# A hybrid decoder layer on one core: w_down with more row pairs in seven products, and sums of weights made by accumulating DMAs

## The chip, the cores and the metric

The kernel runs on one core of one Trainium2 chip. The metric is the device time of one execution in microseconds; the median of three runs of the kernel before is 1053.51 us (1053.41 to 1053.66). TensorE (PE) multiplies, VectorE (DVE), ScalarE (ACT) and GpSimd (POOL) prepare its operands and take up its results, and SyncE (SP) issues nearly all DMAs. All arithmetic is in float32. A product in that precision is made of three matmuls: each operand is split into a high part (a cast to the float32r type) and a low part (the rest), and high × high, high × low and low × high are added.

## The reference

One decoder layer over x of shape (1, 256, 2048): a mixer with two attention groups, then a GeGLU block. Cut to its frame:

```python
h = rmsnorm(x, pre_mix_g)
proj = h @ w_in                               # 2048 x 4368
o_a = swa_sink_attention(q_a, k_a, v_a, sinks)        # 16 heads, window 128, ALiBi, sinks
o_b = forgetting_attention(q_b, k_b, v_b, log_f)      # 16 heads, forget gates
mix = concat(rmsnorm(o_a), rmsnorm(o_b)) @ w_out      # 2048 x 2048
x = x + rmsnorm(mix, post_mix_g)
h = rmsnorm(x, pre_ffn_g)
u = causal_dwconv(h @ w_up, conv_w, conv_b)           # 2048 x 11264, width 3
gate, val = split(u, 2)
y = (gelu(gate) * val) @ w_down                       # 5632 x 2048
x = x + rmsnorm(y, post_ffn_g)
```

The change is about the last product, y, with K = 5632 (44 row blocks of 128), 256 tokens (two blocks of 128) and 2048 columns (four blocks of 512).

## The kernel before, in words

**The stages in time.** Input projection and attention fill the first 240 us, w_out the time to about 340 us. The feed-forward block runs in two halves of 22 row blocks of w_down each: up-projections (359 to 577 us, then w_down's first half to 688 us; up-projections to 928 us, then w_down's second half to the end).

**The weights' path.** A unit of weights, 128 x 1024 float32 (512 KB), is loaded by SP into one of five `raw` buffers (`w_load`, line 69 on). ScalarE casts it to the high part, VectorE subtracts to get the low part (`split`, lines 319 to 321; `w_split`, lines 119 and 122); both parts stand in one of five `wpair` buffers until TensorE has used them. A load waits for its buffer's last reader, a split for its load and its buffer, TensorE for the split.

**w_down.** In each half, 11 pairs of row blocks meet two pairs of column blocks (n = 0 and n = 2). A plain pair (`four`, line 1132, once for each of the two column blocks) makes the eight block products of a 2 x 2 by 2 x 2 block product. A pair in seven products (`seven`, line 1084) makes seven by Winograd's form of Strassen's algorithm: it multiplies sums of blocks of the activations with sums of blocks of the weights and folds the products into y afterwards (`fold`, line 1139). Each block product is three matmuls of 512 columns (`products`, line 1070; its matmul is line 1072).

The table `SEVENS` has an entry for each half and column pair; its length is how many of the 11 pairs go in seven products, and each number says beside which plain pair that one is placed. If two stand at one place, the first half of the first one comes ahead of the plain pair, its other half behind it, and the second one follows whole.

**The sums of activations** are made by POOL when a group of the up-projection is done (lines 1030 to 1033), split, and kept in `sums` (a 4096-column tile, tag "x") with the rest in the tile `more` (tag "gb1").

**The sums of weights** of a pair come about in two ways. On the spot: `seven` loads the four blocks as `top` and `low`, and after w11, w21 and w22 have been split, VectorE makes four sums in place (line 1105), which are split in turn. Or out of DRAM: for the pairs in `STORED`, `stage` (line 909) loads the four blocks during the up-projections in two halves of 256 columns, VectorE makes the sums with four subtractions of 256 columns (line 928), and SP stores them to a DRAM tile `t_dram`. `seven` then loads three of the original blocks and all four sums, the second half of the sums into a buffer of its own, "two" (tag "gb0"), outside the last stage.

**The order of the work.** TensorE's order is written out. `tick()` counts places in TensorE's program, and `later(n, f)` has f issue its instructions n ticks on. There are 8 ticks in a projection, 2 in each unit of w_out (8 in each chunk of 512 columns), and 12 in each of the three parts of the value projection. The other engines' orders are set by a planner, except where instructions are held to the program's order (`keep_in_program_order`) and in stages where all of an engine's order is written out. Each engine runs its instructions in order, and SP's DMA instructions wait in order too.

**Where things live.** The tag "y" is a place of 4096 columns, used in turn by the scratch rows of attention (`scr`), w_out's result (`mix_sb`), four rooms for staging in the first half (`four_of`), and `y_sb`. Three buffers `u` take the up-projection's rows ahead of the convolution.

Of the kernel before, what the change touches and what calls it, by code (L numbers as in the profile page):

```python
# [27 lines left out]
SEVENS = (((0, 0, 1, 1, 2, 2), (0, 0, 1, 1, 2, 2)), ((0, 0, 1, 1, 2), (0, 1, 2)))  # L28
STORED = (((0, 0, 1), (0, 0, 3), (0, 0, 5), (0, 2, 1), (0, 2, 3), (0, 2, 5), (1, 0, 1)), ((1, 0, 3), (1, 2, 0), (1, 2, 1), (1, 2, 2)))
# [5 lines left out]
def hybrid_layer(ctx: ExitStack, tc: tile.TileContext, x, pre_mix_g, w_in, b_forget, sinks,  # L35
# [28 lines left out]
    def later(n, f):  # L64
        todo.setdefault(now[0] + n, []).append(f)
# [257 lines left out]
    with tc.tile_pool(name="mixp", bufs=1) as mp:  # L323
# [33 lines left out]
        scr = main.tile([P, 2 * D], F32, tag="y", name="scr")  # L357
        rowk, rowq, dist, u0, u1 = (scr[:, i * 256:(i + 1) * 256] for i in range(5))
        rot = [0]

        def scratch():
            rot[0] += 1
            i = 6 + rot[0] % 10
            return scr[:, i * 256:(i + 1) * 256]
# [38 lines left out]


# [262 lines left out]
        def cumsum():  # L667
# [3 lines left out]
            cT = scr[0:H, 1280:1536]  # L671
# [33 lines left out]
        mix_sb = main.tile([P, 2, D], F32, tag="y", name="mix_sb")  # L705
        mix = [[mix_sb[:, t, n * 512:(n + 1) * 512] for n in range(4)] for t in range(2)]
# [146 lines left out]
    with tc.tile_pool(name="ffn", bufs=1) as fp:  # L853
# [22 lines left out]
        NU = 3  # L876
# [3 lines left out]
        fp.tile([P, 8], F32, tag="gap", name="gap")  # L880
# [3 lines left out]
        def rows_of(b):  # L884
            u = ubuf[cnt[0] % NU]
            cnt[0] += 1
            if type(b) is list:
                for m, x in enumerate(b):
                    c = fp.tile([P, 256], F32, tag="cs", bufs=1, name="cs")
# [17 lines left out]
        in_dram = {}  # L907

        def stage(half, n, u, start, step, room):

            k = half * FHALF + u * 2
            t = in_dram[half, n, u] = tc.dram_tile([P, 4, 512], F32, name="t_dram")
            src = w_down[k * P:(k + 2) * P, n * 512:(n + 2) * 512].rearrange(
                "(a p) (b c) -> p a b c", p=P, b=2)
            for i, j in enumerate((slice(0, 256), slice(256, 512))):
# [8 lines left out]
                def add(b=b):  # L924
                    b11, b12, b21, b22 = (b[0][:, i, :] for i in range(4))
                    for y, p, q in ((b11, b12, b11), (b12, b22, b12), (b22, b22, b11),
                                    (b21, b21, b22)):
                        tc.keep_in_program_order(dve.tensor_tensor(y, p, q, op=ALU.subtract))
# [49 lines left out]
        for half in range(2):  # L978
# [5 lines left out]

            def sums_at(u):
                w, at = 384 if u < least else 512, 768 * min(u, least) + 1024 * max(u - least, 0)
                if not u:
                    sums.append(main.tile([P, 4096], F32R, tag="x", name="sums"))
# [318 lines left out]
```

## Time and profile before

| | |
|---|---|
| median of three runs | 1053.51 us (1053.41 to 1053.66) |
| the profiled execution | 1053.3 us, its span 1051.4 us |
| mean granted TensorE clock | 0.997 |
| TensorE busy | 1040.0 us, 99% |
| VectorE, ScalarE, GpSimd busy | 80%, 60%, 16% |
| read from HBM, written | 221.86 MB, 15.75 MB |
| DMA | 227 GB/s over the span, 69.5% of 16 engines on SP's queue |

The time of an execution is a little longer than the span between the first and the last instruction. A group line gives line, engine, operation, output<-inputs, shapes and count, then busy us and the mean ns of one, then the engine's idle time just before it and what ended that. "TensorE busy" counts matmuls whose ends are modelled and which overlap; how dense the work is, the distance between their starts tells. A row by stages gives the stage, its length, the busy time of PE, PEld (weight loads), DVE, ACT and POOL with their counts of instructions, the granted clock, the mean busy share of the 16 DMA engines and the GB/s that they moved.

### The profile page before, as it was taken

The numbers are of one execution on the slowest core, as the hardware profiler recorded it, in microseconds if no ns is written. First come the engines' busy times: TensorE is split into PE (matmuls) and PEld (weight loads), VectorE is DVE, ScalarE is ACT, GpSimd is POOL, SyncE is SP. The second block draws the span as 40 slices with busy tenths as digits, with TensorE's granted clock in tenths as the row PEclk, the third lists the DMA queues.
The fourth block names the chain that finished last, engine by engine and source line by source line (L and its number), as shares of the span: only waits on it lengthen the run. The fifth ranks groups of instructions, "written<-read, shape, count | busy, mean of one in ns | idle before, by whom it ended". The sixth has DMA issues, their size and how long they took to land.

```text
span 1051.4 us, 19021 instructions
## 1 busy us (share of the span) xinstructions
PE 1040.0 (99%) x7240; PEld 958.0 (91%) x7240; DVE 837.2 (80%) x1365; ACT 626.9 (60%) x1025; POOL 166.5 (16%) x210
## 2 busy tenths in 40 slices
PE   9999999999999999999999999999999999999996
PEld 7899988888888999999999888899999999988886
DVE  5999877887467888888877988967788777799783
ACT  6777757667557655555555655645565455566561
POOL 3253245441122210100000000000111000000023
PEclk9999999999999999999999999999999999999998
DMA  8645557555874878888875886777677776767783
GB/s 292 199 129 168 182 159 214 164 180 171 294 248 153 255 252 294 287 264 273 283 232 170 263 269 226 244 233 239 220 235 246 226 244 219 236 216 246 244 306 115
DMA packets 187335, 238.98 MB, mean 227 GB/s; under 512 B 8268, under 2 KB 154988, under 8 KB 186348
## 3 DMA queue, kind: packets, MB, share of 16 engines
q1 hardware_dynamic: 186924, 237.37, 69.5%
q8 instruction: 57, 0.93, 0.3%
q10 hardware_dynamic: 320, 0.40, 0.1%
q14 instruction: 34, 0.28, 0.1%
HBM read 221.86 MB, written 15.75 MB: 226 GB/s over the span
## 4 chain that ended last, share of the span: by engine, by line
PE 90%; DVE 4%; ACT 2%; DMA 1%; POOL 1%; issue 1%; SPq 0%; DVEq 0%; POOLq 0%; ACTq 0%
PE bank_att L300 23%; PE bank_acc L300 21%; PE bank_acc L1072 15%; PE bank_acc L317 12%; PE bank_acc L263 5%; PE bank_att L1072 5%; PE bank_acc L270 3%; DVE wpair L122 1%; PE bank_att L317 1%; POOL scr L450 1%; PE bank_att L518 1%; DMA raw<-in_w_in_dram 1%; PE bank_att L483 1%; PE bank_att L527 1%; DMA x_in<-in_x_dram 1%
## 5 line engine op out<-in xcount | busy, mean ns | idle before, releaser
L122 DVE TENSOR_TENSOR wpair<-raw,wpair 128x1024 fp32r<-128x1024 f32 (+3 forms) x317 | 383.6, 1225 | 116.9 <-ACT wpair L119 115.8
L119 ACT CAST wpair<-raw 128x1024 fp32r<-128x1024 f32 (+3 forms) x316 | 320.3, 1032 | 155.6 <-issue 62.6
L300 PE MATMUL bank_att<-hT,wpair 128*128 128x256 f32 x2112 | 241.2, 276 | 0.0
L300 PEld LDWEIGHTS bank_att<-hT,wpair 128*128 128x128 f32 x2112 | 240.4, 188 | 0.2
L300 PE MATMUL bank_acc<-hT,wpair 128*128 128x256 f32 x1920 | 219.2, 276 | 0.0
L300 PEld LDWEIGHTS bank_acc<-hT,wpair 128*128 128x128 f32 x1920 | 218.3, 188 | 0.0
L1072 PE MATMUL bank_acc<-wpair,G 128*128 128x512 f32 x636 | 153.5, 389 | 0.0
L1072 PEld LDWEIGHTS bank_acc<-wpair,G 128*128 128x128 f32 x636 | 119.1, 188 | 24.5
L263 PE MATMUL bank_acc<-hT,wpair 128*128 128x512 f32 x384 | 94.9, 394 | 0.0
L263 PEld LDWEIGHTS bank_acc<-hT,wpair 128*128 128x128 f32 x384 | 69.5, 188 | 13.2
L317 PE MATMUL bank_acc<-wpair,oT 128*128 128x512 f32 x336 | 78.0, 391 | 0.0
L317 PEld LDWEIGHTS bank_acc<-wpair,oT 128*128 128x128 f32 x336 | 62.6, 188 | 12.8
L1030 POOL TENSOR_TENSOR s<-yy 128x128 f32<-128x128 f32 x11 | 7.5, 681 | 408.1 <-DVE yy L1019 408.1
L320 ACT CAST wpair<-raw 128x1024 fp32r<-128x1024 f32 (+1 forms) x54 | 48.0, 892 | 36.2 <-PE bank_acc L1072 17.6
L321 DVE TENSOR_TENSOR wpair<-raw,wpair 128x1024 fp32r<-128x1024 f32 (+1 forms) x54 | 55.0, 1023 | 14.3 <-ACT wpair L320 13.4
L899 ACT ACTIVATE yy<-u,cw 128x256 f32<-128x256 f32 x88 | 48.4, 596 | 20.4 <-DVE u L894 15.3
L270 PE MATMUL bank_acc<-hT,wpair 128*128 128x256 f32 x384 | 49.4, 280 | 0.0
L270 PEld LDWEIGHTS bank_acc<-hT,wpair 128*128 128x128 f32 x384 | 47.4, 188 | 1.4
L317 PE MATMUL bank_acc<-wpair,hT 128*128 128x384 f32 (+1 forms) x288 | 47.7, 321 | 0.0
L317 PEld LDWEIGHTS bank_acc<-wpair,hT 128*128 128x128 f32 x288 | 45.4, 188 | 0.1
L320 ACT CAST G<-yy 128x256 fp32r<-128x256 f32 x44 | 16.0, 406 | 46.8 <-POOL yy L1031 23.9
L901 DVE SCALAR_TENSOR_TENSOR yy<-u,cw,yy 128x256 f32<-128x256 f32 x88 | 39.1, 482 | 2.4 <-ACT yy L899 2.2
(253 smaller groups left out, 1204.9 us busy)
## 6 DMA issues: line engine op xcount, KB each, us to landing
raw<-in_w_up_dram SPq DMA_DIRECT2D x176, 512.0 KB, 4.6
raw<-in_w_down_dram SPq DMA_DIRECT2D x68, 512.0 KB, 5.1
raw<-in_w_in_dram SPq DMA_DIRECT2D x51, 512.0 KB, 5.3
raw<-in_w_out_dram SPq DMA_DIRECT2D x32, 512.0 KB, 4.1
staged<-in_w_down_dram SPq DMA_DIRECT2D x44, 256.0 KB, 5.5
t_dram<-staged SPq DMA_DIRECT2D x22, 512.0 KB, 3.2
raw<-t_dram SPq DMA_DIRECT2D x14, 512.0 KB, 3.7
raw<-in_w_in_dram SPq DMA_DIRECT2D x16, 384.0 KB, 3.4
```

The costliest lines, as they stand in the source:

```text
L119: i1 = act.copy(hi[:, cs], raw[:, cs])
L122: i2 = dve.tensor_tensor(lo[:, cs], raw[:, cs], hi[:, cs].bitcast(F32), op=ALU.subtract)
L263: pe.matmul(b, hi[:, a, m * P:(m + 1) * P], hT[:, kt, 0:512], start=(kt == 0), stop=(last == (0, kt)))
L270: pe.matmul(b[:, 256:512], lo[:, a, m * P:(m + 1) * P], hT[:, u * 4 + a, 0:256], start=False, stop=(last == (1, u * 4 + a)))
L300: pe.matmul(b[:, m * 256:(m + 1) * 256], ws[:, a, m * P:(m + 1) * P], hT[:, kt, i * 256:(i + 1) * 256], start=not begun, stop=last == (low ...
L317: pe.matmul(b, a, r[:, cols], start=(first and i == 0), stop=(last and i == 2))
L320: act.copy(hi, src)
L321: dve.tensor_tensor(lo, src, hi.bitcast(F32), op=ALU.subtract)
L450: pool.tensor_tensor(dst, dst, row, op=ALU.mult)
L899: act.activation(y, u[:, 2:258], AF.Identity, bias=cw[:, 3, ch:ch + 1], scale=cw[:, 2, ch:ch + 1])
L901: dve.scalar_tensor_tensor(y, u[:, 1:257], cw[:, 1, ch:ch + 1], y, op0=ALU.mult, op1=ALU.add)
L1072: pe.matmul(b, x, r, start=b not in opened and not i, stop=closes and i == 2)
```

## The change

- `SEVENS`: 8, 8, 6 and 3 pairs in seven products instead of 6, 6, 5 and 3. In the first half four sevens stand at each of the first two places.
- 19 of these 25 take the weights' sums from DRAM, instead of 11 of 20. Ten (`MADE`, all of the first half) are staged as before, but 7 ticks apart instead of 10, in three rooms instead of four, and with three additions instead of four subtractions. The second half stages nothing any more.
- Nine (`ADDED`: seven of the second half, and the eighth pair of each column pair of the first) are made without an engine's arithmetic: SP copies the four blocks from w_down into the DRAM tile with two DMAs, and three DMAs issued from POOL add (`accum_op`) first the blocks' second column onto the first, then one sum onto a block, then that onto another. The steps are 8 ticks apart, the nine chains 17, from early in attention on.
- The form of the algorithm has its signs changed, so that the weights' sums are sums only; the differences go to POOL's sums of activations and to `fold`. The count of instructions there stays the same.
- The place of y is two tiles, of 3072 columns (tag "y") and of 1024 ("yb"); scratch, mix and y go through a helper, `y_place`. The first half's eighth sum of activations stands in "yb", the seventh (and the second half's sixth) in a new tile "gb2".
- Two buffers `u` instead of three; the tiles "cs" and "last" take the tag "s"; the tile "gap" is 16 columns instead of 8.

```diff
-SEVENS = (((0, 0, 1, 1, 2, 2), (0, 0, 1, 1, 2, 2)), ((0, 0, 1, 1, 2), (0, 1, 2)))
-STORED = (((0, 0, 1), (0, 0, 3), (0, 0, 5), (0, 2, 1), (0, 2, 3), (0, 2, 5), (1, 0, 1)), ((1, 0, 3), (1, 2, 0), (1, 2, 1), (1, 2, 2)))
+SEVENS = (((0, 0, 0, 0, 1, 1, 1, 1), (0, 0, 0, 0, 1, 1, 1, 1)), ((0, 0, 1, 1, 2, 2), (0, 1, 2)))
+MADE = tuple((0, n, u) for n in (0, 2) for u in (0, 1, 3, 4, 6))
+ADDED = tuple((1, 0, u) for u in (1, 3, 4, 5)) + tuple((1, 2, u) for u in range(3)) + ((0, 0, 7), (0, 2, 7))
...
+        def added(at, start):
+            t = in_dram[at] = tc.dram_tile([P, 4, 512], F32, name="t_dram")
+            src = corners(*at)
+            def copy():
+                for a in range(2):
+                    tc.keep_in_program_order(sp.dma_start(t[:, 2 * a:2 * a + 2, :], src[:, a]))
+            def add(to, what):
+                return lambda: tc.keep_in_program_order(
+                    pool.dma_start(to, what, accum_op=ALU.add))
+            for d, f in ((0, copy), (8, add(t[:, 0:2, :], src[:, :, 1, :])),
+                         (16, add(t[:, 3, :], t[:, 0, :])), (24, add(t[:, 2, :], t[:, 3, :]))):
+                later(start + d, f)
+        for i, at in enumerate(ADDED):
+            added(at, 12 + i * 17)
...
-        NU = 3
+        NU = 2
...
-                    b11, b12, b21, b22 = (b[0][:, i, :] for i in range(4))
-                    for y, p, q in ((b11, b12, b11), (b12, b22, b12), (b22, b22, b11),
-                                    (b21, b21, b22)):
-                        tc.keep_in_program_order(dve.tensor_tensor(y, p, q, op=ALU.subtract))
+                    x = b[0]
+                    for y, p, q in ((x[:, 0:2], x[:, 0:2], x[:, 1:4:2]),
+                                    (x[:, 3], x[:, 3], x[:, 0]), (x[:, 2], x[:, 2], x[:, 3])):
+                        tc.keep_in_program_order(dve.tensor_tensor(y, p, q, op=ALU.add))
...
-                    pool.tensor_tensor(s1, a21, a22, op=ALU.add)
+                    pool.tensor_tensor(s1, a21, a22, op=ALU.subtract)
                     pool.tensor_tensor(s2, s1, a11, op=ALU.subtract)
-                    pool.tensor_tensor(s4, a12, s2, op=ALU.subtract)
+                    pool.tensor_tensor(s4, a12, s2, op=ALU.add)
...
-                        start = stage(*at, start, 19 if half else 10, room)
+                        start = stage(at, start, 7, lambda: rooms.append(rooms[0]) or rooms.pop(0))
...
-                    for y, p, q in ((b11, b12, b11), (b12, b22, b12), (b22, b22, b11),
+                    for y, p, q in ((b11, b11, b12), (b12, b12, b22), (b22, b22, b11),
                                     (b21, b21, b22)):
-                        made = dve.tensor_tensor(y, p, q, op=ALU.subtract)
+                        made = dve.tensor_tensor(y, p, q, op=ALU.add)
...
-                    dve.tensor_tensor(y12, d, y22, op=ALU.add)
+                    dve.tensor_tensor(y12, d, y22, op=ALU.subtract)
                     dve.tensor_tensor(y21, f, y22, op=ALU.add)
-                    dve.tensor_tensor(y22, d, y21, op=ALU.add)
+                    dve.tensor_tensor(y22, d, y21, op=ALU.subtract)
```

More of the change, by code (lines that the diff above doesn't have):

```diff
@@ L354, in x_square, with y_place, at @@
                                    accum_out=sqx[t][:, c:c + 1]))
-        scr = main.tile([P, 2 * D], F32, tag="y", name="scr")
-        rowk, rowq, dist, u0, u1 = (scr[:, i * 256:(i + 1) * 256] for i in range(5))
+        def y_place(name):
+            parts = {}
+            def at(t, cs):
+                f, n = t * D + cs.start, cs.stop - cs.start
+                i = f >= 3 * UNIT
+                if i not in parts:
+                    parts[i] = main.tile([P, (1 if i else 3) * UNIT], F32, tag="yb" if i else "y",
+                                         name=name)
+                f -= 3 * UNIT * i
+                return parts[i][:, f:f + n]
+            return at
+        scr = y_place("scr")
+        rowk, rowq, dist, u0, u1 = (scr(0, slice(i * 256, (i + 1) * 256)) for i in range(5))
         rot = [0]
@@ L704, in hybrid_layer @@
         later(stages(5, 1)[2] + 5, lambda: group_rstd(1, rstd_b))
-        mix_sb = main.tile([P, 2, D], F32, tag="y", name="mix_sb")
-        mix = [[mix_sb[:, t, n * 512:(n + 1) * 512] for n in range(4)] for t in range(2)]
+        mix_at = y_place("mix_sb")
+        mix = [[mix_at(t, slice(n * 512, (n + 1) * 512)) for n in range(4)] for t in range(2)]
         def out_half(half, evac, chunks):
@@ L905, in conv, with stage @@
             return y
[L907 to L914, printed above, removed]
+        def stage(at, start, step, room):
+            t = in_dram[at] = tc.dram_tile([P, 4, 512], F32, name="t_dram")
+            src = corners(*at)
             for i, j in enumerate((slice(0, 256), slice(256, 512))):
@@ L1039, in hybrid_layer @@
                     split(*parts, s[:, :w])
-                if not g:
-                    if half:
-                        room = lambda: fp.tile([P, 4, 256], F32, tag="gb0", name="staged")
-                    else:
-                        four_of = main.tile([P, 4, 4, 256], F32, tag="y", name="staged")
-                        rooms = [four_of[:, i] for i in range(4)]
-                        room = lambda: rooms.append(rooms[0]) or rooms.pop(0)
+                if not half and not g:
+                    three_of = main.tile([P, 3 * UNIT], F32, tag="y", name="staged")
+                    rooms = [three_of[:, i * UNIT:(i + 1) * UNIT].rearrange(
+                        "p (a c) -> p a c", a=4) for i in range(3)]
                     start = 0
-                    for at in STORED[half]:
-                        start = stage(*at, start, 19 if half else 10, room)
+                    for at in MADE:
+                        start = stage(at, start, 7, lambda: rooms.append(rooms[0]) or rooms.pop(0))
             if half == 1:
@@ L1096, in seven @@
                 s2, s3, s4, s1 = [
-                    [x[:, i * P:i * P + P] for x in sums[1 + u]] if i < 3 or u >= least
-                    else parts_of(u * 2, 1) for i in range(4)]
+                    sums_of(u, i) if i < 3 or u >= least else parts_of(u * 2, 1)
+                    for i in range(4)]
                 (w11,) = split_into(w_parts(UNIT, held=False), top, 1)
@@ L1273, in hybrid_layer @@
                 r = rstd_y(1, 4, v)
-            gained(last if h else y_sb[:, 1, 1536:1792], b1[h], halves[h])
+            gained(last if h else y_at(1, slice(1536, 1792)), b1[h], halves[h])
         for i, n in enumerate((512, 512, 512, 256, 256)):
```

56 lines of the change are left out of this document (35 added, 21 removed).

## The prediction

> **What bounds the kernel now.** I read the page's busy shares first, then the chain of waits, then a table of busy time by stage, then the groups of single stages. The first two lines are the page's; the rest is the chain in order of time (start, length, what).
>
> ```profile
> span 1051.4 us, 19021 instructions
> ...
> PE 1040.0 (99%) x7240; PEld 958.0 (91%) x7240; DVE 837.2 (80%) x1365; ACT 626.9 (60%) x1025; POOL 166.5 (16%) x210
> ```
>
> ```profile
> 359.35 21.79 PE bank_att L300 x192
> 381.14 21.76 PE bank_acc L300 x192
> ...
> 648.40 6.80 PE bank_acc L1072 x30
> 655.20 2.04 PE bank_att L1072 x9
> ```
>
> TensorE sets the end nearly everywhere. From 359 us on, each pair of up-projections takes 21.76 us for 192 matmuls, again and again, and in the w_down stage 30 matmuls of 512 columns take 6.80 us: 0.2267 us each, with no gap between the pieces. So a matmul of w_down removed is worth 0.2267 us, and any stall that the change creates is paid in full. What counts then is how much room the engines that feed TensorE have. The table by stage shows it (columns: stage, its length, busy time of PE, PEld, DVE, ACT and POOL with instructions, clock, DMA share, GB/s):
>
> ```profile
> 128.00:240.00 112.00, 111.63 (x699) 96.39 (x698) 90.78 (x190) 75.13 (x162) 52.83 (x65) 1.00 0.58 180
> 240.00:320.00 80.00, 80.00 (x381) 66.45 (x380) 49.73 (x75) 47.09 (x80) 13.19 (x11) 1.00 0.68 230
> 320.00:359.00 39.00, 38.33 (x272) 35.15 (x271) 32.35 (x73) 29.45 (x73) 8.84 (x13) 1.00 0.67 219
> 359.00:577.00 218.00, 218.00 (x1923) 217.95 (x1922) 181.66 (x288) 121.45 (x171) 17.72 (x26) 1.00 0.79 256
> 403.00:446.00 43.00, 43.00 (x382) 43.00 (x381) 36.85 (x59) 24.33 (x34) 5.25 (x8) 1.00 0.85 276
> ...
> 490.00:533.00 43.00, 43.00 (x382) 43.00 (x381) 34.67 (x57) 23.71 (x32) 0.00 (x0) 1.00 0.88 282
> 555.00:577.00 22.00, 22.00 (x195) 22.00 (x195) 17.42 (x27) 11.45 (x16) 0.00 (x0) 1.00 0.46 153
> 577.00:688.50 111.50, 111.50 (x494) 92.32 (x494) 99.80 (x113) 68.36 (x74) 0.00 (x0) 1.00 0.77 255
> ...
> 984.00:1006.00 22.00, 22.00 (x99) 18.22 (x98) 16.61 (x18) 15.31 (x21) 0.00 (x0) 1.00 0.78 273
> ```
>
> VectorE is at 90% in w_down's first half (99.80 of 111.50 us) and at 83% in the up-projections before it (181.66 of 218). The DMA engines are at 0.85 to 0.88 while sums are staged (403 to 533 us) and at 0.58 to 0.68 in attention and w_out. Everything keeps up, and two resources have 10 to 15% left.
>
> **What it removes.** A pair in seven products does one block product less than a pair in eight, and a block product is 3 matmuls. SEVENS goes from 6+6+5+3 = 20 pairs to 8+8+6+3 = 25: 5 × 3 × 0.2267 = 3.40 us off TensorE, 2.72 of it in the first half, 0.68 in the second. The number of folds stays four, with the same number of instructions.
>
> **What it adds on VectorE and ScalarE in w_down.** The rows of that stage (line, engine, operation, shapes, count, busy us, mean ns):
>
> ```profile
> L321 DVE TENSOR_TENSOR wpair<-raw,wpair 128x1024 fp32r<-128x1024 f32 x18 | 22.0, 1222 | 7.6 <-ACT wpair L320 7.1
> ...
> L321 DVE TENSOR_TENSOR wpair<-raw,wpair 128x512 fp32r<-128x512 f32 x11 | 7.5, 685 | 0.0
> ...
> L1105 DVE TENSOR_TENSOR raw<-raw 128x512 f32<-128x512 f32 x5 | 3.5, 690 | 0.1
> ```
>
> A pair in seven with sums from DRAM splits one piece of 512 columns and three of 1024: 0.69 + 3 × 1.22 = 4.35 us of VectorE per 21 × 0.2267 = 4.76 us of TensorE. With sums made on the spot four additions of 0.69 come on top: 7.1 us. A plain pair costs 2 × 1.22 = 2.44 us per 24 × 0.2267 = 5.44 us. Per column pair of the first half the change turns two plain pairs into sevens (+2 × 1.91 us) and makes two pairs on the spot instead of three (-2.76 us): +1.06 us. Twice that gives 99.8 + 2.1 = 101.9 us of VectorE in 111.5 - 2.7 = 108.8 us of TensorE: 94%. It still fits, but the sevens now stand four to a group, with only one plain pair beside them: three from DRAM, one on the spot, one plain make 3 × 4.35 + 7.1 + 2.44 = 22.6 us of VectorE in 24.5 us. The five buffers of split weights let VectorE run about one seven ahead; a seven on the spot overdraws its own 4.76 us by 2.3, and the next seven from DRAM returns only 0.4. In the middle of a group that lead covers it: nothing. The first group also carries the tail of the last up-projection:
>
> ```profile
> 577.00:592.60 15.60, 15.60 (x70) 12.89 (x70) 15.13 (x22) 11.63 (x15) 0.00 (x0) 1.00 0.82 277
> 592.60:607.60 15.00, 15.00 (x68) 12.43 (x67) 13.24 (x15) 9.62 (x11) 0.00 (x0) 1.00 0.79 259
> ```
>
> The same mixture of pairs took 15.13 us with that tail and 13.24 without: 1.9 us. On 22.6 that makes 24.5 of 24.5 us. Its bounds are 0 and 1.9; I take 0, since the sevens that open the group now come from DRAM.
>
> **The second half of the loaded sums** goes into one buffer, "two", so its load is issued only when the one before has been split, and all later loads queue behind it on SP. Timeline, chain and DMA issues (median us to landing) of before:
>
> ```profile
> 600.84 1.06 ACT L320 CAST wpair<-two 128x1024 fp32r<-128x1024 f32 x1 [0.26 <-PE bank_att L1072]
> ...
> 601.93 1.23 DVE L321 TENSOR_TENSOR wpair<-two,wpair 128x1024 fp32r<-128x1024 f32 x1
> ...
> 603.18 0.33 SPq L74 DMA_DIRECT2D two<-t_dram  x1
> ```
>
> ```profile
> 602.84 1.36 PE bank_acc L1072 x6
> 604.20 2.04 PE bank_att L1072 x9
> ```
>
> ```profile
> raw<-t_dram SPq DMA_DIRECT2D x14, 512.0 KB, 3.7
> ...
> two<-t_dram SPq DMA_DIRECT2D x8, 512.0 KB, 6.2
> ```
>
> The issue at 603.18 follows the split's end at 603.16. TensorE reads that piece in the last 3 of the 9 matmuls, from 605.56: 2.4 us later. Before, two such sevens never stood side by side in the first half; now the seventh and the eighth pair do, in both column pairs. The next use comes 4.76 us after, so 2.4 + 4.76 less cast (1.06) and split (1.23) leaves 4.9 us for the landing. Measured are 3.7 and 6.2: late by 0 to 1.3 us, twice. The 6.2 was behind another load; here the loads ahead of it are issued earlier, so I take 0.3 twice: 0.6 us. With the first group, the bounds of the whole w_down stage are 0 and 4.5.
>
> **DMA in w_down.** A seven from DRAM loads 1.75 MiB (1.84 MB) per 4.76 us, one on the spot or a plain pair 1.05 MB. The new group moves 3 × 1.84 + 2 × 1.05 = 7.6 MB in 24.5 us: 311 GB/s. The stage's row prices the engines at 255 / 0.77 = 331 GB/s: 94%. In 984 to 1006 us 273 GB/s cost nothing. I add nothing.
>
> **Staging in the up-projections.** Ten pairs (20 half steps) instead of seven, all in the first half, a half step every 7 ticks instead of 10; a tick is 1.36 us there (16 in 21.76).
>
> ```profile
> L928 DVE TENSOR_TENSOR staged<-staged 128x256 f32<-128x256 f32 x56 | 24.1, 429 | 1.0
> ...
> L321 DVE TENSOR_TENSOR sums<-s,sums 128x384 fp32r<-128x384 f32 x5 | 2.8, 558 | 0.9 <-ACT sums L320 0.9
> ```
>
> VectorE: three additions (0.69 for the one of 512 columns, two of 0.43) 20 times are 31.0 us instead of 24.1, and two more splits of sums 1.1: 189.7 of 218 us, 87%. DMA: 1.05 MB per half step over 9.5 us instead of 13.6 is 110 GB/s instead of 77; beside the weights' 524 KB per 2.72 us, 193 GB/s, that makes 303 GB/s where 276 to 282 took 0.85 to 0.88, that is 320 to 325 GB/s at full share: 94%. Rooms come round after 21 ticks, five ticks (6.8 us) after their store, which lands in 3 us. I take nothing; if the 6% weren't there, a missing 3% of 190 us would be 5.7. The second half loses its staging, 8 × 1.72 us of VectorE, which gains nothing, since TensorE sets that stage.
>
> **The sums made by DMA.** Nine pairs: two copies of 512 KB on SP, then three accumulating DMAs on POOL's queue (512, 256, 256 KB), 8 ticks apart, each waiting for the one before; 18 and 27 issues, between 60 and 320 us. No accumulating DMA and no DMA on POOL's queue is in the trace. Nearest rows:
>
> ```profile
> t_dram<-staged SPq DMA_DIRECT2D x22, 512.0 KB, 3.2
> ```
>
> ```profile
> L450 POOL TENSOR_TENSOR scr<-scr 128x256 f32<-128x256 f32 x22 | 24.4, 1131 | 56.7 <-DVE scr L449 36.5 <-DVE rs L505 20.2
> ...
> L587 POOL TENSOR_SCALAR p<-cb,cq 128x256 f32<-128x256 f32 x16 | 12.5, 784 | 2.3 <-DMA cb<-c_dram 2.3
> ```
>
> At 230 / 0.68 = 338 GB/s the 1.05 MB copied take all engines 3.1 us. The 1.05 MB added take at least as long and, as two reads and a write, at most three times that, 9.3. A chain starts every 17 ticks: 29.8 us in attention (64 ticks in 112 us), 23.1 in w_out. So the share rises there from 0.58 to 0.79 to 1.00, in w_out from 0.68 to 0.95 to 1.22. I take the store's price (lower end), since it is the nearest row: then it fits, and costs nothing on the path. On POOL an issue costs between SP's 0.33 and a tensor operation's 1.13 us: 9 to 31 us over 260, beside 52.83 of 112 busy. Behind a POOL DMA that waits stand the multiplications of q and k (L450) and the tables (L587), which the scores need; but POOL idled 56.7 us ahead of L450 alone, and 8 ticks are 11 to 14 us where a 512 KB transfer lands in 3 to 6. Nothing again.
>
> [...]
>
> **Nothing else.** Two buffers u instead of three: a buffer is written again a whole up-projection (10.88 us) after its convolution. Scratch, mix and y in two tiles, and "cs" in "s", change names and dependencies of work long done.
>
> **Sum.** Span 1051.4 - 3.4 + 0.6 = 1048.6. The profiled run took 1053.3, 1.9 outside the span: 1050.5. The median of the runs, 1053.51, lies 0.2 above it: 1050.7 us.
>
> **Rivals.**
> 1. *w_down takes most of it back.* Groups of four sevens overrun VectorE or wait for "two". For it: 94% of VectorE, 94% of DMA, adjacency. Against: no gap at 90% before. Price 2 to 4 us: 1052 to 1054.
> 2. *The accumulating DMAs starve TensorE (slower).* In w_out the share passes 1 once the additions take more than about 4.3 us a chain (0.68 × 23.1 + 3.1 + 4.3 = 23.1). At 9.3 us the surplus is 0.22 × 80 = 18 us of DMA work; the five raw buffers of 512 KB hold 7.8 us of it at 338 GB/s, and 10 remain: 1053.5 - 3.4 + 0.6 + 10 = 1060.7. [...] A POOL that waits for late additions in attention would cost as much through the scores.
> 3. *Staging at 7 ticks saturates the DMA engines* from 360 to 550 us: up to 5.7 us, 1056.4. For and against it stands the fullest stretch of before:
>
> ```profile
> 381.00:403.00 22.00, 22.00 (x197) 22.00 (x196) 19.62 (x33) 12.05 (x18) 2.43 (x4) 1.00 0.96 306
> ```
>
> Little lies above 306 GB/s, but TensorE had no gap in it.
> 4. *Nothing comes off TensorE.* Then 1053.5; against it stands the constant 0.2267.
>
> **How the numbers follow.** A measurement tells about 0.2% from no change, 2.1 us: faster is below 1051.4, slower above 1055.6. Forecast 0.52 (1050.1 to 1051.4), rival 1 0.21, rival 2 0.16 (0.03 of it near no change), rival 3 0.10 (half slower), rival 4 0.01. Faster 0.52, same 0.21 + 0.03 + 0.05 + 0.01 = 0.30, slower 0.13 + 0.05 = 0.18. The gain can't exceed 3.4 us, so the range begins at 1049.8 with the runs' scatter; it ends at 1056.5, where rival 3 does and rival 2 mostly lies beyond. The likeliest case alone: 1049.8 to 1051.4.
>
> **What would show it.** Right: w_down's first half 2.7 us shorter, its matmuls still 0.2267 us apart; 21.76 us per pair of up-projections; DMA share below 0.95 from 240 to 320 us; accumulating DMAs that land within 8 ticks. Wrong: TensorE gaps between the last two sevens of a column pair (rival 1), ScalarE waiting for raw or POOL for t_dram before 320 us (rival 2), ScalarE waiting for raw between 360 and 550 us (rival 3).

## The result, and the profile after

The changed kernel takes 1080.43 us in the median of four runs (1077.53 to 1084.63); the kernel before, on the same chip, 1053.53 (1053.41 to 1053.66). The ratio is 1.0258, with a 95% interval of 1.0218 to 1.0299: 2.6% slower, where 0.3% faster was forecast. The profiled execution took 1078.17 us. The page of after:

```profile
span 1076.5 us, 19099 instructions
...
PE 1046.6 (97%) x7225; PEld 959.6 (89%) x7225; DVE 835.2 (78%) x1338; ACT 632.2 (59%) x1038; POOL 198.4 (18%) x248
...
q0 software_dynamic: 5040, 9.44, 5.8%
...
PE 67%; DVE 11%; DMA 10%; ACT 4%; issue 4%; POOL 3%; SPq 0%; DVEq 0%; POOLq 0%; ACTq 0%
```

The q0 line is new: the packets of POOL's DMAs. The chain that sets the end now runs for a tenth of the span through DMAs. Where the 25 us were lost, one row tells: that of the up-projection matmuls of one of its two banks, which begins with the first half's up-projections and ends with the second half's (ns min/median/max, then first and last start in us). Before, then after:

```profile
L300 PE MATMUL bank_att<-hT,wpair x2112: 276/276/282, 359.2 to 927.6; 128*128 128x256 f32 x192
```

```profile
L301 PE MATMUL bank_att<-hT,wpair x2112: 276/276/282, 376.9 to 952.9; 128*128 128x256 f32 x192
```

Three parts of the span follow, and all later runs are read in this way. The **front** (projections, attention, w_out) ends at the first start: 376.9 - 359.2 = 17.7 us later. The **middle** (both up-projections and w_down's first half) lasts from first to last start: 576.0 us, not 568.4. The **end** (w_down's second half) is the rest of the span: 123.6, not 123.8. In the chain of after the middle splits again:

```profile
377.06 21.79 PE bank_att L301 x192
398.85 21.76 PE bank_acc L301 x192
...
551.17 21.76 PE bank_att L301 x192
```

The up-projections keep their 21.76 us, so the middle's 7.6 us, and the 2.7 that should have come off there, were lost in w_down's first half. The stages by busy time (columns as before) show the same two places:

```profile
128.00:240.00 112.00, 107.79 (x658) 92.76 (x657) 84.08 (x181) 70.37 (x152) 53.80 (x68) 0.97 0.86 239
240.00:357.00 117.00, 109.21 (x555) 92.02 (x553) 70.18 (x119) 66.61 (x131) 34.73 (x37) 0.96 0.80 234
...
421.00:490.00 69.00, 69.00 (x611) 69.00 (x610) 61.85 (x94) 38.21 (x55) 8.47 (x12) 1.00 0.94 303
490.00:545.00 55.00, 55.00 (x488) 55.00 (x486) 49.44 (x79) 29.83 (x43) 7.95 (x12) 1.00 0.93 310
...
595.00:714.00 119.00, 111.97 (x483) 89.38 (x482) 99.89 (x113) 71.64 (x82) 0.00 (x0) 1.00 0.79 264
```

TensorE idles 12.0 of 229 us in the front and 7.0 of 119 in w_down, and not at all while sums are staged, although the DMA engines stand at 0.93 and 0.94 there. In the front the granted clock is 0.97 and 0.96.

### The profile page after: what moved, and what is told of

Its sections match the earlier page's. It is cut to its first block, busy times and chain, and to the rows that moved or that the text cites. A ratio compares the mean times of both kernels' runs of the same rounds, so it can differ in the third digit from the quotient of the medians.

```text
span 1076.5 us, 19099 instructions
## 1 busy us (share of the span) xinstructions
PE 1046.6 (97%) x7225; PEld 959.6 (89%) x7225; DVE 835.2 (78%) x1338; ACT 632.2 (59%) x1038; POOL 198.4 (18%) x248
## 3 DMA queue, kind: packets, MB, share of 16 engines
q0 software_dynamic: 5040, 9.44, 5.8%
## 4 chain that ended last, share of the span: by engine, by line
PE 67%; DVE 11%; DMA 10%; ACT 4%; issue 4%; POOL 3%; SPq 0%; DVEq 0%; POOLq 0%; ACTq 0%
PE bank_att L301 22%; PE bank_acc L301 20%; PE bank_acc L1119 8%; PE bank_acc L318 5%; PE bank_acc L264 3%; DVE wpair L123 3%; DMA t_dram<-in_w_down_dram 3%; DMA two<-t_dram 3%; DMA raw<-in_w_out_dram 3%; DVE wpair L322 2%; PE bank_att L1119 2%; PE bank_acc L271 2%; PE bank_att L318 1%; ACT wpair L120 1%; POOL scr L493 1%
## 5 line engine op out<-in xcount | busy, mean ns | idle before, releaser
L123 DVE TENSOR_TENSOR wpair<-raw,wpair 128x1024 fp32r<-128x1024 f32 (+3 forms) x307 | 375.0, 1239 | 116.0 <-ACT wpair L120 114.9
L120 ACT CAST wpair<-raw 128x1024 fp32r<-128x1024 f32 (+3 forms) x306 | 307.8, 1031 | 122.9 <-issue 43.2
L1119 PE MATMUL bank_acc<-wpair,G 128*128 128x512 f32 x546 | 135.5, 390 | 1.8 <-DVE wpair L322 1.0
L1119 PEld LDWEIGHTS bank_acc<-wpair,G 128*128 128x128 f32 x546 | 101.9, 188 | 24.2 <-DVE wpair L123 1.8
L321 ACT CAST wpair<-raw 128x1024 fp32r<-128x1024 f32 (+1 forms) x72 | 63.6, 900 | 44.2 <-DMA raw<-t_dram 8.6
L322 DVE TENSOR_TENSOR wpair<-raw,wpair 128x1024 fp32r<-128x1024 f32 (+1 forms) x72 | 73.2, 1035 | 17.7 <-ACT wpair L321 17.7
L1119 PE MATMUL bank_att<-wpair,G 128*128 128x512 f32 x141 | 40.6, 393 | 1.6 <-DVE wpair L322 1.4
```

The costliest lines, as they stand in the source:

```text
L120: i1 = act.copy(hi[:, cs], raw[:, cs])
L123: i2 = dve.tensor_tensor(lo[:, cs], raw[:, cs], hi[:, cs].bitcast(F32), op=ALU.subtract)
L321: act.copy(hi, src)
L322: dve.tensor_tensor(lo, src, hi.bitcast(F32), op=ALU.subtract)
L1119: pe.matmul(b, x, r, start=b not in opened and not i, stop=closes and i == 2)
```

## The experiments

What ends the waits in the front? POOL's timeline of after (start, length, idle time before and its releaser), its row among the waits, and the chain:

```profile
163.33 0.87 POOL L439 DMA_DIRECT2D t_dram<-t_dram  x1 [6.14 <-DMA t_dram<-in_w_down_dram]
...
255.09 0.86 POOL L439 DMA_DIRECT2D t_dram<-t_dram  x1 [7.70 <-DMA t_dram<-in_w_down_dram]
```

```profile
POOL t_dram L439 <- DMA t_dram<-in_w_down_dram: 24.8, 4, 9.8
...
ACT keys L321 <- POOL scr L493: 24.3, 8, 9.6
...
PE bank_att L526 <- ACT keys L321: 8.1, 2, 5.1
```

```profile
148.29 14.75 DMA t_dram<-in_w_down_dram
163.33 0.87 POOL t_dram L439
164.20 0.77 POOL scr L493
165.45 2.93 PE bank_att L526 x24
...
246.22 8.58 DMA t_dram<-in_w_down_dram
255.09 0.86 POOL t_dram L439
```

The first addition of this chain takes 14.75 us to land; POOL stands before the second one, behind it the multiplication of keys (L493), behind that ScalarE's cast of them, and then TensorE's scores. So for the front there were two theories: **POOL's waits** (a late addition holds the keys behind it: L493 follows at 164.20, after a wait of 6.14 us), and **the additions' DMA time** (weights arrive late, whoever waits). For w_down there were three: the single buffer **"two"**, VectorE's **additions on the spot** inside the groups of sevens, and the ring of five **raw** buffers.

All runs in one table: total in us, ratio to before with its 95% interval, and the three parts of the profiled execution. "No chains" means that the nine chains are left out and their pairs read other sums. The runs of one of these kernels lie 1 to 7 us apart, those of before 2.1 at most, and the profiled execution is one of them: x1 (no chains), x2 (copies only) and x13 (plain copies spread) run the same w_down code and have middles of 581.7, 579.7 and 578.6, the changed kernel 576.0. A difference in the middle of less than some 6 us is therefore read from the totals. Only after, x3, x4, x14, b1 and b2 compute the whole layer; the other kernels leave work out or put other work in its place. x15, x16, x17 and b2 ran on another chip than the other experiments; each ratio is to the kernel before on the same chip, which took 1053.45 to 1053.56 in every series.

| run | total (lowest to highest) | ratio [95%] | front | middle | end |
|---|---|---|---|---|---|
| before | 1053.53 (1053.41 to 1053.66) | | 359.2 | 568.4 | 123.8 |
| after | 1080.43 (1077.53 to 1084.63) | 1.0258 [1.0218, 1.0299] | 376.9 | 576.0 | 123.6 |
| x1_no_chains | 1066.09 (1063.45 to 1068.63) | 1.0119 [1.0100, 1.0137] | 360.5 | 581.7 | 124.7 |
| x2_copies_only | 1063.93 (1061.39 to 1064.98) | 1.0095 [1.0080, 1.0110] | 359.9 | 579.7 | 123.6 |
| x3_spread | 1071.00 (1070.37 to 1074.80) | 1.0178 [1.0159, 1.0197] | 367.5 | 577.8 | 123.4 |
| x5_plain_copies | 1073.96 (1070.58 to 1075.05) | 1.0182 [1.0157, 1.0207] | 370.7 | 578.2 | 124.4 |
| x13_spread_plain | 1063.35 (1060.97 to 1067.60) | 1.0098 [1.0064, 1.0132] | 359.6 | 578.6 | 124.2 |
| x4_two_buffers | 1073.77 (1070.98 to 1075.01) | 1.0188 [1.0173, 1.0204] | 378.2 | 571.2 | 123.4 |
| x9_no_spot_sums | 1055.08 (1053.65 to 1058.12) | 1.0017 [1.0007, 1.0026] | 359.6 | 569.7 | 123.3 |
| x8_low_elsewhere | 1067.84 (1065.65 to 1071.57) | 1.0128 [1.0109, 1.0146] | 360.0 | 582.0 | 127.9 |
| x11_two_low | 1067.84 (1065.27 to 1069.30) | 1.0132 [1.0113, 1.0151] | 359.8 | 578.9 | 128.9 |
| x12_spot_first | 1072.62 (1070.01 to 1074.64) | 1.0174 [1.0156, 1.0192] | 359.7 | 587.7 | 125.5 |
| x14_spread_first | 1078.76 (1076.94 to 1082.02) | 1.0244 [1.0219, 1.0269] | 366.8 | 584.4 | 124.0 |
| x15_first_two | 1051.88 (1050.69 to 1055.30) | 0.9987 [0.9978, 0.9996] | 359.7 | 570.8 | 123.1 |
| x16_first_raw | 1065.95 (1065.31 to 1066.67) | 1.0116 [1.0102, 1.0130] | 358.4 | 582.6 | 123.8 |
| x17_two_nosum | 1052.44 (1051.29 to 1054.04) | 0.9987 [0.9978, 0.9997] | 360.7 | 568.5 | 123.1 |
| b1_best | 1066.22 (1064.71 to 1068.52) | 1.0123 [1.0107, 1.0140] | 360.5 | 582.5 | 123.7 |
| b2_two | 1053.41 (1051.33 to 1054.84) | 0.9995 [0.9986, 1.0004] | 359.7 | 567.2 | 123.2 |

### The front: chains left out, or only their copies

```diff
# x1_no_chains
-        for i, at in enumerate(ADDED):
-            added(at, 12 + i * 17)
+                    for k, at in enumerate(ADDED):       # after the staging of MADE
+                        in_dram[at] = in_dram[MADE[k]]
# x2_copies_only: each chain is only its two copies
+            for d, f in ((0, copy),):
```

> The changed kernel without its nine chains: neither the copies on SP nor the accumulating DMAs on POOL. Those nine pairs read the sums of the first nine staged pairs instead, so their part of y is not the layer's. Everything from the up-projections on is the same work. Both theories of the first part (A: POOL waits in its order for an accumulating DMA that lands late, and q and k behind it reach the scores late; B: the chains take the DMA bandwidth that the weights need) expect the 17.7 us lost before the up-projections to vanish. If the 10.2 us lost in w_down's first half (119.1 us instead of 108.8) has causes of its own, 1060 to 1063 us, with w_down's first half still at 117 to 120 us. If the chains cause that one too, 1050 to 1051 us.

> The changed kernel with the copies on SP (9.4 MB) but without the 27 accumulating DMAs, so nine pairs use unsummed blocks of weights and y is not the layer's. A: no POOL wait, so the first part is as in the kernel before: 1060 to 1063 us. B, if the copies count: they are about a third of the chains' DMA time, so a third or more of the 17.7 us stays: 1066 us or more.

Without chains the front is back to 360.5, with SP's copies alone 359.9, both within 1.3 us of before. So the copies cost nothing there that can be told, and POOL's DMAs cost all the rest. The middle stays as slow: w_down's loss does not come from the chains. Both totals lie above the 1060 to 1063 us expected, since w_down lost more than the 10.2 us of the changed kernel's profiled execution.

### The front: later steps, or plain copies in the additions' place

```diff
# x3_spread: steps 16 ticks apart instead of 8
-            for d, f in ((0, copy), (8, add(...)), (16, add(...)), (24, add(...))):
+            for d, f in ((0, copy), (16, add(...)), (32, add(...)), (48, add(...))):
# x5_plain_copies: the same DMAs on POOL's queue, without the addition
-                    pool.dma_start(to, what, accum_op=ALU.add))
+                    pool.dma_start(to, what))
# x13_spread_plain: both
```

> The whole layer; the steps of a chain are 16 ticks apart instead of 8, the same DMAs of the same size. A: a DMA of POOL's queue then finds its forerunner landed (it takes 8.6 to 14.8 us where 16 ticks are 22 to 28), POOL does not wait, and at most 3 of the 17.7 us stay: 1061 to 1066 us. B: the bytes per time are nearly the same, so at least half of it stays: 1069 us or more.

> The changed kernel with the 27 DMAs on POOL's queue as plain copies: same places, sizes and waits, but they overwrite instead of adding, so nine pairs use blocks instead of sums and y is not the layer's. F: it is the adding (a second read of the destination) that makes them slow and costly: the software queue's share falls from 5.8% to about 3% (1.05 MB a chain at a copy's 3.1 us instead of 6.9), the 512 KB ones land in 5 to 7 us instead of 8.6 to 14.8, POOL hardly waits, and the part before the up-projections comes to within 4 us of the kernel before: 1063 to 1068 us. [...]

> Steps 16 ticks apart and plain copies instead of accumulating ones (nine pairs use blocks instead of sums). In the part before the up-projections the changed kernel loses 17.7 us, with spread steps 8.3, with plain copies 11.5, without additions 0.7. If the loss is POOL's waits plus the DMA time of the additions, this one has neither the first nor half of the second: 0 to 4 us remain, total 1060 to 1067. If SP and POOL issues or the copies' bandwidth make the rest, 7 or more remain: 1069 or more.

End of the front in us, before 359.2:

| | steps 8 ticks apart | 16 apart |
|---|---|---|
| DMAs that add | 376.9 (+17.7) | 367.5 (+8.3) |
| the same DMAs as plain copies | 370.7 (+11.5) | 359.6 (+0.4) |

Each theory had its part, and neither is the whole. With both causes away the loss is gone; each alone still costs 8.3 or 11.5 us. These are single profiled executions, but the medians of the totals say the same: after is 9.4 us above x3 and 6.5 above x5, and x13 is 7.7 below x3 and 10.6 below x5. In x5 POOL still waits, though its DMAs of 512 KB land in 7.0 us in the median, not 11.5 (waits up to the end of w_out, and the queue's row):

```profile
POOL t_dram L439 <- DMA t_dram<-in_w_down_dram: 20.7, 4, 6.5
...
ACT keys L321 <- POOL scr L493: 19.4, 8, 7.7
```

```profile
q0 software_dynamic: 2736, 9.44, 3.1%
```

The queue's rows give the price of the addition. After: 5.8% of 1076.5 us are 62.4 us of all 16 engines for nine chains, 6.9 us a chain. As plain copies the same 9.44 MB take 3.1% of 1073.3 us, 3.7 a chain. An addition costs 1.9 times a copy, 62.4 against 33.3 us for all nine chains.

In x3 POOL's additions wait 8.4 us in all, where in after it is 50.7 (10.6 of them put down to a load of w_out); what is left is late weights. Its stages, and its chain in w_out:

```profile
128.00:240.00 112.00, 109.96 (x685) 93.54 (x684) 88.83 (x186) 74.67 (x160) 58.35 (x72) 1.00 0.90 256
240.00:357.00 117.00, 112.83 (x600) 95.08 (x600) 78.09 (x136) 72.28 (x149) 30.97 (x31) 1.00 0.82 244
```

```profile
276.06 16.93 DMA raw<-in_w_out_dram
...
295.42 11.01 DMA raw<-in_w_out_dram
```

A load of w_out lands after 11 and 17 us. Its median in the whole trace, 4.1 us before, tells the same of after:

```profile
raw<-in_w_out_dram SPq DMA_DIRECT2D x32, 512.0 KB, 7.1
...
t_dram<-in_w_down_dram POOLq DMA_DIRECT2D x9, 512.0 KB, 11.5
```

The mean share in x3 is 0.90 and 0.82, not 1: TensorE starves at less than a full mean. The work comes in clusters: from 280 to 300 us the share is 1.07 and 1.02 in stretches of 10 us, for 287 and 231 GB/s, and in the next 10 us TensorE is busy for 7.33. In x13 the same bytes without the arithmetic make 0.83 and 0.78, and TensorE is as busy as before in both stages; the first one's row:

```profile
128.00:240.00 112.00, 111.58 (x701) 96.54 (x700) 91.40 (x190) 74.95 (x161) 58.19 (x76) 1.00 0.83 248
```

### w_down: one buffer "two", and what stands in a group

The chain of after goes through "two" five times within 90 us (three of them shown):

```profile
608.41 0.61 DVE raw L1152
609.05 0.70 DVE low L1152
609.77 0.70 DVE low L1152
...
615.68 1.23 DVE wpair L322
616.92 6.59 DMA two<-t_dram
...
677.31 6.93 DMA two<-t_dram
...
697.75 6.60 DMA two<-t_dram
...
704.44 1.05 ACT wpair L321
705.52 1.24 DVE wpair L322
```

One buffer is free again after load, cast (1.05) and split (1.24), so a round takes 8.9 to 9.2 us in the three shown (the other two loads took 5.81 and 5.48), where two sevens from DRAM side by side need one every 4.76 us. The first lines show how the causes meet: the third pair's additions (L1152) stand on the chain ahead of the split that frees "two" at 616.91, and only then is the fifth pair's load issued.

```diff
# x4_two_buffers (the whole layer): "two" in turn in two places
-   own = None if tail else fp.tile([P, UNIT], F32, tag="gb0", name="two")
+   own = None if tail else fp.tile([P, UNIT], F32, name="two", **(
+       {"tag": "yy", "bufs": 2} if len(opened_by) % 2 else {"tag": "gb0"}))
+   opened_by.append(u)
# x9_no_spot_sums (no chains): the four additions of a pair on the spot are left out, with a dependency of the first
-   made = dve.tensor_tensor(y, p, q, op=ALU.add)
+   pass
# x17_two_nosum: x9 with the two buffers of x4
```

> The changed kernel, the whole layer, with the loads of the sums' second half going in turn into the buffer of before and into one of the two yy buffers, so that SP can issue each a pair earlier. C: w_down's first half loses its 10.2 us because SP stands at the load into the one buffer, with all later loads behind it: then at least 7 come back, w_down's first half takes 109 to 112 us, in all 1068 to 1074 us. D: VectorE's or the DMA engines' load in groups of four sevens sets it: 117 us or more in that stage, and no change of the total beyond the scatter of 1077 to 1085.

> Without the nine chains, and the four additions of VectorE are left out in each pair with sums made on the spot (4 x 2.76 = 11 us of VectorE in w_down's first half), so those pairs too use unsummed blocks. D: VectorE's load sets the stage: it falls from 124.8 us to 115 or less, the total to 1053 to 1057. E: no change beyond the scatter, 119 to 125 us and 1062 to 1069 in all, as loads are what is late.

> Without the nine chains, groups as in the changed kernel, two buffers for "two", and without the additions on the spot (those pairs use unsummed blocks). If the round of "two" and VectorE's additions are the two causes there are, the stage comes to its floor: 108.8 to 110 us, total 1049.5 to 1052, for the first time below the kernel before. If a third one is there (the DMA engines at 94%), 112 us or more.

Against x17, which has neither cause, one buffer costs 2.6 us (x9: 1055.08 against 1052.44). The additions alone cost some 2 to 3, an estimate: x4's 1073.77 (1074.52 in the profiled execution) less the 19.0 us that the latter's front lost is 1054.8 (1055.5). Both together cost 13.7 (x1: 1066.09). So they are not additive. The reading that fits, and that the chain above bears out: a pair on the spot in the middle of a group overdraws VectorE, and the lead that it eats is the one that a late "two" would need. Part of the 13.7 is TensorE's clock: in x1's profiled execution TensorE waits 2.44 us near the end of the stage, and the granted clock is 0.63 from 691 to 697 us and 0.80 to 703. That is worth 6 × 0.37 + 6 × 0.20 = 3.4 us, an estimate; in the w_down of x9, x4 and x17 the clock stays at 1.00. The DMA engines don't set the stage: x17 moves the same bytes there, at a share of 0.85 and 286 GB/s. Still, x17 and x15 lie 2.3 and 1.8 us above the 1050.1 that the removed matmuls alone would give (1053.5 - 3.4), which was not explained. In the whole layer the second buffer brings 6.7 us (1080.43 to 1073.77).

The ring of raw buffers was tried by taking a load out of it (`low` of the sevens from DRAM in a place of its own), alone and with two buffers:

```diff
# x8_low_elsewhere, and x11_two_low with x4's buffers (no chains in both)
-   low = w_load(w_rows(...), 1, 1024)[0]
+   low = w_load(w_rows(...), 1, 1024, raw=fp.tile([P, UNIT], F32, tag="yy", bufs=2, name="low"))[0]
```

> Without the nine chains (as in the first of these runs, whose w_down first half took 124.8 us where 108.8 is the floor and whose total was 1063.5 to 1068.6; same part of the sums left out), and the lower row block of a pair with sums from DRAM is loaded into the yy buffers, not into raw. E: the five raw buffers set w_down's first half: a buffer comes round in landing, cast and split, 6 + 1.1 + 1.2 = 8.3 us, but sevens from DRAM side by side use three in 4.76 us, five in 7.9. With two of three left it takes 119 us at most, the total 1056 to 1061. D: VectorE's work in groups of four sets it: no change, 1063 to 1068.

> Without the nine chains; the second half of the loaded sums goes in turn to its own buffer and to yy, and the lower row blocks go to yy. E and C together (raw buffers, and SP standing at the one buffer two): w_down's first half 109 to 114 us, total 1050 to 1055. D: as the first of these runs, 119 us or more, 1063 to 1068. If yy's two buffers, now used by both, become the narrow place in their turn, it lies between.

Both take 1067.84, no better than x1's 1066.09: fewer loads in the ring didn't help. But the place chosen made a wait of its own, as a row of x11's w_down stage shows, and their ends are 3.2 and 4.2 us longer than x1's, so these two runs don't clear the ring:

```profile
ACT wpair L321 <- DMA low<-in_w_down_dram: 17.7, 6, 4.0
```

### w_down: the pairs on the spot at the head of the group

Then the order. `MADE` without u = 0 and 4 makes those two pairs the ones on the spot: the first of each group of four.

```diff
# x12_spot_first (no chains); x14_spread_first: the same in x3, the whole layer
-MADE = tuple((0, n, u) for n in (0, 2) for u in (0, 1, 3, 4, 6))
+MADE = tuple((0, n, u) for n in (0, 2) for u in (1, 2, 3, 5, 6))
# x15_first_two: x12 with the two buffers of x4
# x16_first_raw: x12 with the second half of the sums through the raw buffers
-   own = None if tail else fp.tile([P, UNIT], F32, tag="gb0", name="two")
+   own = None
```

> Without the nine chains (same part of the sums left out as in the first run), and the two pairs with sums made on the spot stand first in their groups (the first and the fifth pair instead of the third and the sixth), so that their two halves lie around the plain pair, as in the kernel before. VectorE has the same work. H: it is the place that makes the additions stall TensorE, 7.1 us of VectorE within 4.76 us of a seven that has no plain pair inside: then w_down's first half takes 109 to 115 us, the total 1050 to 1057. D': the mere sum of VectorE's work (94%) sets it: 119 to 125 us, 1062 to 1069.

> The whole layer: accumulating chains with steps 16 ticks apart, and pairs on the spot first in their groups. If the two causes are separate and add up: about 8 us lost ahead of the up-projections and 0 to 6 in w_down's first half: 1058 to 1066 us. If spreading or placing works only alone: above 1068.

> Without the nine chains, pairs on the spot first in their groups, and the loads of "two" in turn to its own buffer and to yy. I: the round of the one buffer, 7.3 us, against sevens of 4.76 us side by side, made the 130.8 us; with two buffers it has 9.5 us, and w_down's first half falls to 109 to 115 us, the total to 1050 to 1056. If VectorE's additions or the DMA engines set it, 119 us or more stays.

> Without the nine chains, pairs on the spot first, and the loads of "two" go into the five raw buffers like all others. I: no round of a single buffer any more, but four raw buffers per seven: five come round in 8.3 us where 5.95 are wanted in three sevens side by side, so between: 112 to 122 us, total 1053 to 1063. If something else sets it, 125 us or more stays.

Alone the new order is worse: 1072.62 against 1066.09, and 1078.76 against x3's 1071.00, where a gain was expected of both. It puts three sevens from DRAM side by side, and x12's casts now wait for "two" eight times in w_down:

```profile
ACT wpair L321 <- DMA two<-t_dram: 25.0, 8, 4.3
```

With two buffers the same order is the fastest of this series, 1051.88: the second buffer takes 20.7 us off x12. x16, which has no buffer "two" at all, stays at 1065.95; there more loads go through the five raw buffers, and the casts wait for these:

```profile
ACT wpair L321 <- DMA raw<-in_w_down_dram: 10.8, 9, 3.8
ACT wpair L321 <- DMA raw<-t_dram: 9.2, 12, 3.5
```

So what the changed w_down lacks is a second place for the sums' second half. The number of places alone doesn't tell: x16 has one less than x12 and is faster, and x8 and x11 load into the same buffers as x4 and x15 without a gain. With the second buffer and the pairs on the spot at the head of the groups, their additions cost nothing that can be told: x15 has them, x17 hasn't, 1051.88 and 1052.44.

### A whole layer with these findings

```diff
# b1_best
-SEVENS = (((0, 0, 0, 0, 1, 1, 1, 1), (0, 0, 0, 0, 1, 1, 1, 1)), ((0, 0, 1, 1, 2, 2), (0, 1, 2)))
-MADE = tuple((0, n, u) for n in (0, 2) for u in (0, 1, 3, 4, 6))
-ADDED = tuple((1, 0, u) for u in (1, 3, 4, 5)) + tuple((1, 2, u) for u in range(3)) + ((0, 0, 7), (0, 2, 7))
+SEVENS = (((0, 0, 0, 1, 1, 1, 2), (0, 0, 0, 1, 1, 1, 2)), ((0, 0, 1, 1, 2, 2), (0, 1, 2)))
+MADE = tuple((0, n, u) for n in (0, 2) for u in (1, 2, 4, 5, 6))
+ADDED = (1, 0, 1), (1, 0, 3)                              # two chains 40 ticks apart, steps 16 apart
+LATER = ((1, 0, 5),) + tuple((1, 2, u) for u in range(3))  # staged in the second half's up-projections
# b2_two: b1 with the two buffers of x4
```

> The whole layer, 7, 7, 6 and 3 pairs in seven products (23 instead of 20: 2.04 us less for TensorE). Ten pairs staged in the first half at 7 ticks, four in the second as in the kernel before, two chains only, 40 ticks apart with steps of 16, and pairs on the spot first in their groups. If the causes are POOL's waits, the additions' DMA time and the place of the pairs on the spot, nothing of them is left: 1051 to 1052.5 us, faster than before by 1 to 2. If two chains cost as two ninths of nine (1.8 us with spread steps) it is no change, 1053 to 1054; if groups of sevens cost in themselves, above.

> The whole layer with 7, 7, 6 and 3 pairs, two chains 40 ticks apart with steps of 16, pairs on the spot first (as the run before that took 1066.2 us, 125.6 of it in w_down's first half, floor 110.2) and two buffers for "two". I: 110 to 114 us there, total 1051.5 to 1055. Otherwise as before, 1063 to 1068.

b1 keeps the front (360.5) but not w_down (1066.22, where 1051 to 1052.5 was expected): again one buffer. b2 has no gap left:

```profile
577.00:687.50 110.50, 110.50 (x491) 91.40 (x490) 96.67 (x108) 70.46 (x78) 0.00 (x0) 1.00 0.85 282
```

```profile
L302 PE MATMUL bank_att<-hT,wpair x2112: 276/276/282, 359.7 to 926.9; 128*128 128x256 f32 x192
```

Its middle is 1.2 us shorter than before's, where two more pairs in seven should give 2 × 3 × 0.2267 = 1.36, and the end 0.6 shorter where one more should give 0.68. Yet the median of eleven runs is 1053.41, a ratio of 0.9995 (0.9986 to 1.0004): no change. The profiled run was one of the faster ones, 1051.77. Why the others are slower than it, by up to 3 us, was not settled; no kernel that computes the whole layer was shown to beat the one before.

## Why the prediction was wrong

**Right.** The block products removed do come off: matmuls of w_down still start 0.2267 us apart, and where nothing waits the time is that of the arithmetic (b2, and the second half here). A piece of that second half in the chain of after:

```profile
953.84 6.81 PE bank_acc L1119 x30
```

Staging every 7 ticks was worked out at 303 GB/s and 94% and cost at nothing; measured are 303 GB/s at 0.94 and 310 at 0.93, TensorE without a gap, and VectorE 187.76 us where 189.7 were expected. One reading there was off without harm: the stores land in 7.2 us, not 3, more than the 6.8 us left before their room is used again. Rival 3 (staging saturates the DMA engines) fell. SP's copies of 512 KB cost next to nothing (x2's front ends at 359.9, before's at 359.2). VectorE's sum for w_down, 101.9 us, was right too: 99.89.

**The first failed step** is the price of the additions: "I take the store's price (lower end), since it is the nearest row". 3.1 us a chain were taken, 6.9 measured. The bounds (3.1 to 9.3) held it. The upper one, three times a copy's 3.1, was the author's estimate, and the lower end was chosen because a row lay near it, a store's, with no row of an addition at hand. With the measured value the share is over 1 in w_out by the prediction's own sum, 0.68 + (3.1 + 6.9) / 23.1 = 1.11. It cost 8.3 us in x3, where POOL hardly waits. That sum wasn't the whole mechanism, though. x3's measured share there stayed at 0.82 in the mean, full only in stretches. And rival 2 would have hidden 7.8 us of the surplus, 0.11 × 80 = 8.8 us, in the raw buffers and left 1.0.

**The second** stands in the same paragraph: "POOL idled 56.7 us ahead of L450 alone, and 8 ticks are 11 to 14 us where a 512 KB transfer lands in 3 to 6". The 512 KB addition lands in 11.5 us in the median, 14.75 at 148 us. The steps are 8 ticks apart only in the order of issue: POOL got to the first addition late, at 148.29 us, and stood before the second one at 157.19, 8.9 us later. And the idle time ahead of 22 instructions together is no cover for one wait among them; in before the multiplications of that place ran at 156.99 us with no idle time ahead of them. The waits cost 11.1 us even without the arithmetic (x5's 11.5 less x13's 0.4).

Rival 2 had named both ("starve TensorE", and "a POOL that waits for late additions in attention would cost as much through the scores"), at 10 us and a chance of 0.16. It is what happened, at 17.7. TensorE's clock, which no step priced, added to it. Of the 17.7 us, 11.1 are idle time of TensorE in the front (14.2 us instead of 3.1), and 6.6 are longer busy time (362.7 instead of 356.1). After the waits of 2.97 and 5.13 us the granted clock is 0.54 (165 to 170 us) and 0.50 (257 to 262.4), and after x5's of 3.20 us 0.64 (251.2 to 254.9); in x3's front, where the longest wait is 1.7 us, it stays at 1.00. How much of the 6.6 us is the clock was not isolated: in x3 busy time grew by 3.1 us without it. Nor does the length of one wait tell when the clock falls: in w_down it fell to 0.50 in x15 after waits of 0.81 and 0.75 us close together, and to 0.54 in x14 after 1.34 and 0.76. What length of wait brings it down is open.

**The third** failed term is w_down: "I take 0.3 twice: 0.6 us" for "two", and "In the middle of a group that lead covers it: nothing" for VectorE. The stage was to take 2.1 us less and its middle took 7.6 more: some 10 us, over the stage's upper bound of 4.5. The mechanism for "two" was named (load, cast and split against 4.76 us), but only for the seventh and the eighth pair. By the new `SEVENS` the first and second also stand side by side. On the chain "two" was late five times: for the fifth and the eighth pair of both column pairs, and for the second pair of one. And the two terms were costed one by one, each against the whole lead that the five split buffers give, while the chain shows the additions delaying the split that frees "two": either cause alone costs 2 to 3 us, both together 13.7 (x9, x4, x1 against x17). Rival 1 (w_down takes most back) came about too, beyond its 2 to 4 us.

**Open.** Why the totals of these kernels scatter by up to 7 us: in some the slower runs have a lower mean clock (x8: 1065.65 at 0.998, 1071.57 at 0.995), in others not (x1: 0.994 in all four, 1063.45 to 1068.63). And whether a larger ring of raw buffers would cure w_down as the second "two" does, which was not tried; why b2's other runs lie above the profiled one.

## What to carry to other kernels

A DMA that adds costs nearly two copies in this kernel (6.9 against 3.7 us a chain), and takes 8.6 to 14.8 us to land for 512 KB beside its loads; a step that waits for one belongs far enough after it that it has always landed, or on a queue behind which nothing else stands (not tried here). Where an instruction waits on an engine and others stand behind it (L493 here, behind POOL's wait of 6.14 us), don't sum the engine's idle time: look for the instructions right behind it, and who waits for those. Where two edits live from the same lead, add their overdrafts before comparing with it. A single buffer whose load, cast and split together exceed its period sets the period (8.9 to 9.2 us here against 4.76), even if that happens only when two such uses stand side by side. And a wait of TensorE can cost more than its length, through the clock behind it: after one of 5.13 us here the granted clock was 0.50, then 0.72, and matmuls of 512 columns took 0.28 us instead of 0.2267.

## What the runs showed of the hardware

A POOL DMA costs POOL itself time, and one that adds costs 1.5 to 2 times as much: the 256 KB and the 512 KB issues of after, then those of x5 with plain copies (count, ns min/median/max, first and last start):

```profile
L439 POOL DMA_DIRECT2D t_dram<-t_dram x18: 807/856/888, 78.7 to 329.0; - x18
...
L439 POOL DMA_DIRECT2D t_dram<-in_w_down_dram x9: 1168/1458/1518, 62.1 to 301.4; - x9
```

```profile
L439 POOL DMA_DIRECT2D t_dram<-t_dram x18: 523/564/612, 78.5 to 318.0; - x18
...
L439 POOL DMA_DIRECT2D t_dram<-in_w_down_dram x9: 706/713/916, 62.0 to 294.8; - x9
```

The medians are 0.86 us (256 KB) and 1.46 (512 KB) against 0.56 and 0.71. After one stall TensorE's matmuls were slower for a while: the scores of 256 columns at 257 us start 5.13 us late, and the 24 matmuls of 512 columns that follow take 6.69 us, 0.28 each instead of 0.2267; the granted clock is 0.72 from 262.4 to 266 us and 1.00 behind that.

```profile
257.19 0.58 PE L526 MATMUL bank_att<-keys,qh 64*128 64x256 f32 x2 [5.13 <-ACT keys L321]
...
262.40 6.69 PE L318 MATMUL bank_acc<-wpair,oT 128*128 128x512 f32 x24
```
